# Attention scores by pairs of heads, in the two 64-row halves of the array

## The chip, the cores and the metric

The kernel runs on one core of a Trainium2 chip. The metric is the device time of one execution, in microseconds. Three runs of the kernel before gave 2763.35, 2765.78 and 2760.66 us, with a median of 2763.35 us. One more execution was recorded by the hardware profiler: 2758.38 us in all, of which the recorded span, from the first to the last instruction, is 2756.6 us. All durations below are from that one execution, so sums are made against it, and they are carried to the median by adding 5 us.

## The reference

The kernel computes one layer of an encoder: x is 2048 tokens by 1024 features in float32. A normalised x is multiplied by one large input matrix, which gives the operands of two token mixers (attention and an mLSTM) and two gates. Their outputs are projected, gated, multiplied by `w_out` and added to x; a feed-forward part of width 4096 and a last normalisation follow. The change is in the attention:

```python
# 8 heads of width 64; chunks of 64 tokens; own chunk and the 8 before it
scores = jnp.einsum('bclhd,bckhd->bchlk', qc, kband) * (1.0 / math.sqrt(d))
rel_idx = jnp.clip(rel, -MAX_REL_DIST, MAX_REL_DIST) + MAX_REL_DIST    # 256
scores = scores + rel_bias[:, rel_idx]
p = softmax(where(valid, scores, -1e30))
out = jnp.einsum('bchlk,bckhd->bclhd', p, vband)
```

Keys at a distance of 256 or more all get the same bias of their head, the last column of `rel_bias`.

## The kernel before

The tokens are four blocks of 512. Each matrix product is done with every float32 operand split in two parts, a high one (rounded to TensorE's float32r) and a low one (the remainder), and three products: high by high, high by low, low by high. The large products (`quad`, `product`, `token_tiles`, `down`) are matmuls of 128 rows by 128 columns on 512 moving columns. They use sums of blocks of weights and of activations, which ScalarE (ACT) and VectorE (DVE) form and split.

Every piece of work is a generator, and the class `Flow` runs them all in Python with a clock per engine. A `yield "pe", 500` gives that step's planned duration; the planner always issues the step that could start first by its clocks, and so writes out one fixed order of instructions for each engine. A step that waits for a buffer (`yield "get", pool, n`) or an event waits in this plan. On the chip the engines then run their orders with semaphores. The large products have priority 5 and the attention 1, so the parts of attention are placed between the large products. `mixers(0)` begins the attention of blocks 0 and 1, `mixers(2)` that of blocks 2 and 3.

Within a block, `attention` (L1072) fetches the values of a pair of heads, and then starts `head` for each of the 8 heads. A head's keys and queries come from DRAM by SP's DMA queue (`kfar`, `qfar`); 64 partitions hold the high part of the keys and the other 64 their low part, so that one matmul over 128 rows gives two of the products. The queries stand in both halves. `unit` takes two of the head's four tiles of 128 queries. `scores` (L1265) makes for each tile the products with up to 640 keys, in one or two matmul groups of up to 320 columns, one matmul for the high part of the queries and one for the low part:

```python
for x in range(halves):
    for y in range(2):
        nc.tensor.matmul(bks[x][:, :w], q[:, y, i * P:(i + 1) * P],
                         kf[:, f * P + x * w:f * P + x * w + w], start=y == 0, stop=y == 1)
```

DVE adds the bias and takes the maximum (L1283), ACT the exponential (L1289), and one of the two divides by the sum. `turn` (L1299) transposes the probabilities on TensorE in pieces of up to four 128-blocks (L1308) and splits them (L1311, L1313). `weigh` (L1186) multiplies them by the values (L1201): where a block of keys serves both query tiles, one matmul with 512 moving columns does both, else one with 256. ACT and DVE add the halves of the result (L1212 to L1219), which is then kept in DRAM or split in place.

The bias of a head is a table of 128 by 640 values, read by one DMA from a row of 768 numbers; GpSimd writes -1e30 into two corners (L1118, L1119).

In four places outside the attention `norm_mid` (L1988) adds the squares of a row block by two matmuls with ones, with a tile `part` of its own.

Of the kernel before, what the change touches and what calls it, by code (L numbers as in the profile page):

```python
# [28 lines left out]
P = 128  # L29
# [219 lines left out]
class Layer:  # L249
# [8 lines left out]
    def make_tiles(self, pool, psum):  # L258
# [6 lines left out]
        self.bias = Pool([f32(f"bias{i}", 640) for i in range(2)])  # L265
# [16 lines left out]
        self.part, self.onesr = f32r("part", T), f32r("onesr", 2)  # L282
# [33 lines left out]
    def setup_late(self):  # L316
# [13 lines left out]
        nc.vector.tensor_copy(self.onesr, self.ones)  # L330
        fl.put(self.temp, raw)
# [489 lines left out]
    def dense(self):  # L821
# [36 lines left out]
        for s in range(NS):  # L858
# [212 lines left out]
    def attention(self, b):  # L1071
# [6 lines left out]
        for j in range(4):  # L1078
            vs = yield "get", self.rpool, 1 if b == 0 else 2
# [8 lines left out]
            for i in range(2):  # L1088
                h = 2 * j + i
                k, q = yield "get", self.rpool, 2  # L1090
                fl.spawn(self.head(b, h, vs, k, q), 1)
            if j == 0:
                fl.set(B["begun"])
        fl.set(B["kq_all"])
        yield "wait", B["head_done"]
        fl.put(self.rpool, *pt)
    def head(self, b, h, vs, k, q):
        fl, nc, B = self.fl, self.nc, self.blk[b]
        j, rows = h // 2, slice(h % 2 * 64, h % 2 * 64 + 64)
        kf = k.bitcast(F32)  # L1100
        for n, x in ((0, b - 1), (1, b)):
            if x < 0:
                continue
            yield "wait", [self.k_ev[x, j]]
            yield "sp", 800, 2000
            for a in range(2):
                nc.sync.dma_start(kf[a * 64:a * 64 + 64, n], self.kfar[x].ap()[j, a, rows])
        yield "wait", [self.q_ev[b, j]]
        yield "sp", 800, 2000
        for a in range(2):  # L1110
            nc.sync.dma_start(q.bitcast(F32)[a * 64:a * 64 + 64],
                              self.qfar[b].ap()[j, :, rows].rearrange("a p c -> p a c"))
        (bias,) = yield "get", self.bias, 1
        yield "sp", 1500, 2000
        rb = self.io["rb"]
        nc.sync.dma_start(bias, bass.AP(rb.tensor, h * 768, [[1, P], [1, 640]]))
        yield "pool", 180
        nc.gpsimd.memset(bias[0:64, 0:64], NEG)  # L1118
        nc.gpsimd.memset(bias[64:128, 576:640], NEG)  # L1119
        done = [Event(), Event()]  # L1120
        for u in range(2):
            fl.spawn(self.unit(b, h, u, k, q, bias, done[u]), 1)
        yield "wait", done
        fl.put(self.bias, bias)
        fl.put(self.rpool, k, q)
        B["heads_left"][j] -= 1
        if B["heads_left"][j] == 0:
            fl.put(self.rpool, *vs)
        fl.set(B["head_done"][h])
# [20 lines left out]
    def unit(self, b, h, u, k, q, bias, done):  # L1150
# [3 lines left out]
        prob, evs = {}, []  # L1154
        for n in range(2):
            i = 2 * u + n
            evs.append(Event())
            prob[i] = sct[n]
            fl.spawn(self.scores(b, i, k, q, bias, sct[n], evs[n]), 1)
        first = {i: (4 if b == 0 else i) for i in prob}  # L1160
        i0 = 2 * u
        cols = []
        for kt in range(min(first.values()), i0 + 6):
            use = [i for i in prob if first[i] <= kt <= i + 4]
            cols.append((kt, use))
        cols.sort(key=lambda c: (-len(c[1]), c[0]))
        pieces, room = [], 0
        for c in cols:
            if room < len(c[1]):
                pieces.append([])  # L1170
                room = 4
            pieces[-1].append(c)
            room -= len(c[1])
# [3 lines left out]
        for n, pc in enumerate(pieces):  # L1177
            (slots[n],) = yield "get", B["pt"], 1
            fl.spawn(self.turn(pc, slots[n], prob, first, pev[n]), 1)
        fl.spawn(self.weigh(b, h, u, pieces, slots, pev, done), 1)  # L1180
# [3 lines left out]
    def weigh(self, b, h, u, pieces, slots, pev, done):  # L1184
        fl, nc, B = self.fl, self.nc, self.blk[b]
        i0 = 2 * u  # L1186
        yield "wait", [B["vp_ev"][h // 2]]
# [5 lines left out]
        for pc, sl, ev in zip(pieces, slots, pev):  # L1193
            yield "wait", [ev]
            yield "pe", sum((0, 116, 228)[len(use)] for _, use in pc)
            o = 0
            for kt, use in pc:
                st = self.v_part(b, h, kt)
                c0 = (use[0] - i0) * P
                w = len(use) * P  # L1200
                nc.tensor.matmul(bkv[:, :, c0:c0 + w], st, sl[:, :, o:o + w], start=n == 0,  # L1201
                                 stop=n == total - 1)
                n += 1
                o += w
# [3 lines left out]
        r0 = (h % 2) * 64  # L1208
        own, other = slice(r0, r0 + 64), slice(64 - r0, 128 - r0)
        (tmp,) = yield "get", self.temp, 1  # L1210
        yield "act", act_ns(512, True)
        nc.scalar.copy(tmp[own, :512], bk[other])  # L1212
        yield "dve", dve_ns(512)
        nc.vector.tensor_add(tmp[own, :512], bk[own], tmp[own, :512])  # L1214
        fl.put(self.banks, bk)
        cols = slice(u * 256, u * 256 + 256)
        direct = self.direct(b, h // 2)
        yield "dve", dve_ns(256)
        nc.vector.tensor_add(tmp[own, :256], tmp[own, :256], tmp[own, 256:512])  # L1219
        if direct:  # L1220
            yield "wait", [B["mix_got"]]
            r = B["mix"][h // 2]
            yield "act", act_ns(256)
            nc.scalar.copy(r[own, 0, cols], tmp[own, :256])  # L1224
            yield "dve", dve_ns(256)
            nc.vector.tensor_sub(r[own, 1, cols], tmp[own, :256], r[own, 0, cols].bitcast(F32))  # L1226
            fl.put(self.temp, tmp)
            self.mix_done(b, h // 2)
            fl.set(done)
            return  # L1230
        fl.spawn(self.keep_mix(b, h // 2, self.mixd.ap()[b, h // 2, own, cols], tmp[own, :256], self.temp, tmp), 1)
# [33 lines left out]
    def scores(self, b, i, k, q, bias, sct, ev):  # L1265
        fl, nc = self.fl, self.nc
        e, st = sct
        f = 4 if b == 0 else i
        n = (i + 5 - f) * P
        kf = k.rearrange("p a c -> p (a c)")  # L1270
        halves = 2 if n > 256 else 1
        w = n // halves
        bks = yield "get", self.banks, halves
        yield "pe", 500
        for x in range(halves):
            for y in range(2):
                nc.tensor.matmul(bks[x][:, :w], q[:, y, i * P:(i + 1) * P],  # L1277
                                 kf[:, f * P + x * w:f * P + x * w + w], start=y == 0, stop=y == 1)
        br = bias[:, ::-1]
        j0 = 640 - n  # L1280
        for x in range(halves):
            yield "dve", dve_ns(w)
            nc.vector.tensor_tensor_reduce(  # L1283
                out=e[:, x * w:x * w + w], in0=bks[x][:, :w], in1=br[:, j0 + x * w:j0 + x * w + w],
                op0=ALU.add, op1=ALU.min, scale=-1.0, scalar=st[:, 0:1] if x > 0 else 3e38, accum_out=st[:, x:x + 1])
            fl.put(self.banks, bks[x])
        mx = st[:, halves - 1:halves]
# [11 lines left out]
    def turn(self, piece, slot, prob, first, ev):  # L1299
        fl, nc = self.fl, self.nc  # L1300
        (bk,) = yield "get", self.banks, 1
        n = sum(len(use) for _, use in piece)
        yield "pe~", 108 * n
        o = 0
        for kt, use in piece:
            for i in use:
                c = (kt - first[i]) * P
                nc.tensor.transpose(bk[:, o:o + P], prob[i][0][:, c:c + P], self.ident)  # L1308
                o += P
        yield "act", act_ns(o, True)  # L1310
        nc.scalar.copy(slot[:, 0, :o], bk[:, :o])  # L1311
        yield "dve", dve_ns(o)
        nc.vector.tensor_sub(slot[:, 1, :o], bk[:, :o], slot[:, 0, :o].bitcast(F32))  # L1313
# [674 lines left out]
    def norm_mid(self, s, h):  # L1988
# [9 lines left out]
        yield "act", act_ns(512)  # L1998
        nc.scalar.copy(self.part, tot[:, :512])
        (bk,) = yield "get", self.banks, 1  # L2000
        for x in range(2):
            yield "pe", 227
            nc.tensor.matmul(bk, self.onesr[:, 0:1].to_broadcast([P, P]), self.part, start=x == 0, stop=x == 1,
                             skip_group_check=True)
            if x == 0:
                yield "dve", dve_ns(512)
                nc.vector.tensor_sub(self.part, tot[:, :512], self.part.bitcast(F32))
# [308 lines left out]
    def late(self):  # L2316
        yield from self.setup_late()
        self.fl.set(self.ev_late)

    def build(self):  # L2320
# [15 lines left out]
        self.gated, self.mtd = f32d("gatepart", 40, T), f32d("mrow", NB, MH, T)  # L2336
        self.fin_ev = [E(KT) for _ in range(2)]
# [129 lines left out]
```

## Time and profile before

| | |
|---|---|
| median of three runs | 2763.35 us |
| profiled execution, and its span | 2758.38 us, 2756.6 us |
| TensorE (PE) busy | 2725.7 us, 99% |
| weight loads (PEld) busy | 2265.7 us, 82% |
| VectorE (DVE) busy | 2098.2 us, 76% |
| ScalarE (ACT) busy | 1551.2 us, 56% |
| GpSimd (POOL) busy | 50.4 us, 2% |
| DMA queue of SP, share of 16 engines | 73.3% |
| scores, matmuls (L1277) | 480 |
| values, matmuls (L1201) | 336 |

A line such as "L1277 PE MATMUL bank<-r,r 128\*128 128x320 f32 x384" names the source line, the engine, the operation, what is written and read, the stationary tile (rows\*columns of the array), the moving tile (partitions x columns) and the count. In a group the mean duration of a matmul is from its issue to its end in PSUM; matmuls overlap in the pipeline, so what one costs the engine is the distance from its start to the next one's start, which the timeline gives. PEld is the loading of the stationary tile, which can go on while the matmul before still streams.

### The profile page before, as it was taken

How to read it: one execution, taken by the hardware profiler on the slowest of the kernel's cores; microseconds unless marked ns; L12 is line 12 of the kernel's file. 1: busy time of each engine (PE TensorE's matmuls, PEld its weight loads, DVE VectorE, ACT ScalarE, POOL GpSimd, SP SyncE). 2: the span in 40 equal slices, each digit the busy share in tenths (PEclk: the TensorE clock that was granted, in tenths of full speed). 3: DMA queues.
4: the chain of work that ended last, by engine and by line, in shares of the span. 5: the costliest groups of instructions: out<-in, count | busy, mean ns of one | idle time of the engine just before them, and what ended most of it. 6: DMA issues, size and time to landing. Idle time of an engine off the chain costs nothing.

```text
span 2756.6 us, 38227 instructions
## 1 busy us (share of the span) xinstructions
PE 2725.7 (99%) x12856; PEld 2265.7 (82%) x12856; DVE 2098.2 (76%) x3715; ACT 1551.2 (56%) x2665; POOL 50.4 (2%) x124
## 2 busy tenths in 40 slices
PE   9999999999999999999999999999999999999998
PEld 8878888788888888788888888888788888888887
DVE  7878766788886678897767898788888675667675
ACT  6555456757763435566556776576445565564443
POOL 0000000000000000000000000000000000000000
PEclk9999999999999999999999999999999999999999
DMA  8877678888978898757769876777665464578763
GB/s 296 287 265 258 237 258 279 254 267 275 293 257 272 305 317 305 256 204 262 261 236 295 253 255 213 245 225 259 219 230 178 153 217 154 187 259 276 283 228 129
DMA packets 331145, 682.46 MB, mean 248 GB/s; under 512 B 36708, under 2 KB 61924, under 8 KB 330948
## 3 DMA queue, kind: packets, MB, share of 16 engines
q1 hardware_dynamic: 330804, 680.01, 73.3%
q8 instruction: 101, 1.65, 0.2%
q14 instruction: 96, 0.79, 0.1%
q10 hardware_dynamic: 144, 0.01, 0.0%
HBM read 468.74 MB, written 211.14 MB: 247 GB/s over the span
## 4 chain that ended last, share of the span: by engine, by line
PE 88%; DVE 5%; issue 2%; ACT 2%; DMA 2%; POOL 0%; SPq 0%; POOLq 0%; ACTq 0%; DVEq 0%
PE bank L610 38%; PE bank L541 10%; PE bank L542 10%; PE bank L543 10%; PE bank L641 10%; PE bank L646 2%; PE bank L1201 2%; PE bank L1277 2%; PE bank L1308 2%; DVE wsp L482 1%; ACT wsp L480 1%; PE bank L1551 0%; ACT sc L1289 0%; DVE r L1065 0%; DMA r<-qfar 0%
## 5 line engine op out<-in xcount | busy, mean ns | idle before, releaser
L610 PE MATMUL bank<-r,wsp 128*128 128x512 f32 x4872 | 1113.2, 390 | 2.9 <-DVE ctx L1944 1.2
L610 PEld LDWEIGHTS bank<-r,wsp 128*128 128x128 f32 x4872 | 914.3, 188 | 195.4 <-DVE ctx L1944 1.6
L480 ACT CAST wsp<-wraw 128x1024 fp32r<-128x1024 f32 x453 | 475.8, 1051 | 479.8 <-PE bank L610 192.2
L482 DVE TENSOR_TENSOR wsp<-wraw,wsp 128x1024 fp32r<-128x1024 f32 x453 | 553.4, 1222 | 223.6 <-ACT wsp L480 215.4
L541 PE MATMUL bank<-r,wsp 128*128 128x512 f32 x1152 | 455.1, 395 | 0.4 <-ACT r L1224 0.4
L542 PE MATMUL bank<-r,wsp 128*128 128x512 f32 x1152 | 449.8, 390 | 0.0
L543 PE MATMUL bank<-r,wsp 128*128 128x512 f32 x1152 | 449.5, 390 | 0.0
L641 PE MATMUL bank<-r,wsp 128*128 128x512 f32 x1512 | 369.8, 394 | 1.2 <-DVE tmp L1214 1.2
L641 PEld LDWEIGHTS bank<-r,wsp 128*128 128x128 f32 x1512 | 278.6, 189 | 56.8 <-DVE tmp L1214 1.6
L543 PEld LDWEIGHTS bank<-r,wsp 128*128 128x128 f32 x1152 | 216.4, 188 | 46.1
L541 PEld LDWEIGHTS bank<-r,wsp 128*128 128x128 f32 x1152 | 216.7, 188 | 41.7 <-ACT r L1224 0.8
L542 PEld LDWEIGHTS bank<-r,wsp 128*128 128x128 f32 x1152 | 216.7, 188 | 40.6 <-DVE r L1226 0.2
L1065 DVE TENSOR_TENSOR r<-r 128x512 fp32r<-128x512 f32 x269 | 179.4, 686 | 67.8 <-ACT r L1060 66.6
L1060 ACT CAST r<-r 128x512 fp32r<-128x512 f32 x269 | 162.8, 620 | 110.7 <-DMA r<-u 88.6
L1737 DVE TENSOR_TENSOR ctx<-bank,ctx 128x512 f32<-128x512 f32 x150 | 102.8, 686 | 69.4 <-PE bank L610 69.1
L499 DVE TENSOR_TENSOR wraw<-wraw,wraw 128x1024 f32<-128x1024 f32 x112 | 136.1, 1218 | 1.8 <-DMA wsum<-wraw 0.6
L1289 ACT ACTIVATE sc<-sc,scs 128x640 f32<-128x640 f32 (+4 forms) x128 | 97.4, 761 | 62.6 <-DVE scs L1283 61.6
L1729 ACT COPY ctx<-bank 128x512 f32<-128x512 f32 x150 | 87.2, 582 | 53.6 <-PE bank L610 52.6
L2062 ACT ACTIVATE ctx<-ctx 128x512 f32<-128x512 f32 x96 | 60.5, 630 | 100.6 <-DVE ctx L1737 100.4
L1313 DVE TENSOR_TENSOR r<-bank,r 128x512 fp32r<-128x512 f32 (+1 forms) x168 | 96.5, 593 | 10.2 <-ACT r L1311 9.3
L1201 PE MATMUL bank<-r,r 128*128 128x512 f32 x336 | 97.5, 373 | 2.8 <-DVE r L1313 2.5
L1311 ACT CAST r<-bank 128x512 fp32r<-128x512 f32 (+1 forms) x168 | 80.9, 514 | 22.7 <-PE bank L1308 21.4
(243 smaller groups left out, 2994.5 us busy)
## 6 DMA issues: line engine op xcount, KB each, us to landing
wraw<-in_wf SPq DMA_DIRECT2D x202, 512.0 KB, 4.1
wraw<-wsum SPq DMA_DIRECT2D x120, 512.0 KB, 4.7
r<-u SPq DMA_DIRECT2D x224, 256.0 KB, 4.3
u<-ctx SPq DMA_DIRECT2D x128, 256.0 KB, 2.2
u<-tmp SPq DMA_DIRECT2D x96, 256.0 KB, 2.1
wraw<-in_w SPq DMA_DIRECT2D x47, 512.0 KB, 4.4
ctx<-in_wf SPq DMA_DIRECT2D x88, 256.0 KB, 4.6
wsum<-ctx SPq DMA_DIRECT2D x88, 256.0 KB, 4.0
```

The lines of the kernel that those rows point to most:

```text
L480: nc.scalar.copy(w[:, 0], raw)
L482: nc.vector.tensor_sub(w[:, 1], raw, w[:, 0].bitcast(F32))
L499: V.tensor_sub(dst, x, y)
L541: mm(ps, lh, rh, start=first, stop=False)
L542: mm(ps, lh, rl, start=False, stop=False)
L543: mm(ps, ll, rh, start=False, stop=last)
L610: mm(ps, wv[:, x, k, n], a[:, y], start=new and k == 0 and x == y == 0, stop=k == 3 and x == 1, skip_group_check=True)
L641: mm(ps, wv[:, x, k, n], a[:, y], start=start and x == y == 0, stop=stop and x == 1, skip_group_check=True)
L1060: self.nc.scalar.copy(dst[:, 0], src)
L1065: self.nc.vector.tensor_sub(dst[:, 1], src, dst[:, 0].bitcast(F32))
L1201: nc.tensor.matmul(bkv[:, :, c0:c0 + w], st, sl[:, :, o:o + w], start=n == 0, stop=n == total - 1)
L1737: nc.vector.tensor_add(t[:, o:o + 512], ps, t[:, o:o + 512])
```

## The change

One task now does a pair of heads. The keys' high parts of both heads are one tile (`kh`, head 0 in partitions 0 to 63, head 1 in 64 to 127), the low parts another (`kl`). The scores of a query tile are made for both heads at once: each product is a matmul over 64 rows, head 0 in rows 0 to 63 of the array and head 1 in rows 64 to 127, into two PSUM banks; three products per head. The keys are cut into the nearest 384 and what is left (up to 256), since only the nearest 384 have differing biases: the table loses the last column's value (softmax doesn't change by a constant), so the farther keys need only a mask. The table without that value is made at the start (`late`) and kept in DRAM. The values are weighed by one matmul of 256 moving columns per head and key block. Beside it, `norm_mid` takes a tile of the common pool for its split and has planner priority 0 in place of 3.

```diff
-        self.bias = Pool([f32(f"bias{i}", 640) for i in range(2)])
+        self.bias = Pool([f32(f"bias{i}", 768) for i in range(2)])
+        self.mask = f32("mask", 256)
...
-                        fl.spawn(self.norm_mid(s, h), 3)
+                        fl.spawn(self.norm_mid(s, h), 0)
...
+    def pair(self, b, j, vs, kh, kl, q):
...
+            for a, k in enumerate((kh, kl)):
+                yield "sp", 800, 2000
+                nc.sync.dma_start(k.bitcast(F32)[:, n], self.kfar[x].ap()[j, a])
...
+        nc.sync.dma_start(q.bitcast(F32), self.qfar[b].ap()[j].rearrange("a p c -> p a c"))
...
+        for x in range(2):
+            yield "sp", 1000, 2000
+            nc.sync.dma_start(bias[:, x], bass.AP(rb.tensor, (2 * j + x) * 512, [[1, P], [1, 384]]))
+            yield "pool", 120
+            nc.gpsimd.memset(bias[0:64, x, 0:64], NEG)
...
+        for i in range(NT):
+            fl.spawn(self.unit(b, j, i, kh, kl, q, bias, read[i], done[i]), 1)
...
-            yield "pe", sum((0, 116, 228)[len(use)] for _, use in pc)
...
-                nc.tensor.matmul(bkv[:, :, c0:c0 + w], st, sl[:, :, o:o + w], start=n == 0,
-                                 stop=n == total - 1)
+            yield "pe", 116 * len(pc)
+            for o, (kt, a) in enumerate(pc):
+                nc.tensor.matmul(bkv[:, :, a * P:a * P + P], self.v_part(b, 2 * j + a, kt), sl[:, :, o * P:o * P + P],
+                                 start=n == 0, stop=n == total - 1, skip_group_check=True)
...
-        halves = 2 if n > 256 else 1
...
-        yield "pe", 500
...
+        cuts = [(0, n)] if n <= 384 else [(0, n - 384), (n - 384, n)]
...
+        for x, (c0, c1) in enumerate(cuts):
+            w = c1 - c0
+            bks = yield "get", self.banks, 2
+            yield "pe", 3 * (0.42 * w + 13) + 130
+            for y, (u, v) in enumerate(((0, 0), (0, 1), (1, 0))):
+                for a in range(2):
+                    rows = slice(a * 64, a * 64 + 64)
+                    nc.tensor.matmul(bks[a][:, :w], q[rows, u, i * P:(i + 1) * P],
+                                     kf[v][rows, f * P + c0:f * P + c1], start=y == 0, stop=y == 2)
+            for a in range(2):
+                fl.spawn(self.row_max(n, x, c0, c1, bks[a], bias[:, a], sct[a], maxed[a], evs[a]), 1)
...
+    def late(self):
+        yield from self.setup_late()
+        (tab,) = yield "get", self.temp, 1
+        yield "sp", 60, 2000
+        self.nc.sync.dma_start(tab[:AH, :512], self.io["rb"])
+        yield "dve", dve_ns(512)
+        self.nc.vector.tensor_scalar(tab[:AH, :512], tab[:AH, :512], tab[:AH, 511:512], None, op0=ALU.subtract)
+        yield from self.store(self.rbd.ap(), tab[:AH, :512], Event(), self.temp, tab)
```

(In `late`, the call of `setup_late` is not new.)

More of the change, by code (lines that the diff above doesn't have):

```diff
@@ L1094, in attention @@
         fl.set(B["kq_all"])
-        yield "wait", B["head_done"]
+        yield "wait", B["pair_done"]
         fl.put(self.rpool, *pt)
-    def head(self, b, h, vs, k, q):
+    def pair(self, b, j, vs, kh, kl, q):
         fl, nc, B = self.fl, self.nc, self.blk[b]
-        j, rows = h // 2, slice(h % 2 * 64, h % 2 * 64 + 64)
-        kf = k.bitcast(F32)
         for n, x in ((0, b - 1), (1, b)):
@@ L1104, in head @@
             yield "wait", [self.k_ev[x, j]]
-            yield "sp", 800, 2000
-            for a in range(2):
-                nc.sync.dma_start(kf[a * 64:a * 64 + 64, n], self.kfar[x].ap()[j, a, rows])
+            for a, k in enumerate((kh, kl)):
+                yield "sp", 800, 2000
+                nc.sync.dma_start(k.bitcast(F32)[:, n], self.kfar[x].ap()[j, a])
         yield "wait", [self.q_ev[b, j]]
[L1109 to L1122, printed above, removed]
-        yield "wait", done
[L1124 to L1129, printed above, removed]
+        yield "sp", 1570, 2000
+        nc.sync.dma_start(q.bitcast(F32), self.qfar[b].ap()[j].rearrange("a p c -> p a c"))
+        (tile,) = yield "get", self.bias, 1
+        bias = tile.rearrange("p (a c) -> p a c", a=2)
+        rb = self.rbd.ap()
+        for x in range(2):
[3 more added lines that the diff above has]
+            nc.gpsimd.memset(bias[0:64, x, 0:64], NEG)
+        read, done = [Event() for _ in range(NT)], [Event() for _ in range(NT)]
+        for i in range(NT):
+            fl.spawn(self.unit(b, j, i, kh, kl, q, bias, read[i], done[i]), 1)
+        yield "wait", read
+        fl.put(self.bias, tile)
+        fl.put(self.rpool, kh, kl, q)
+        yield "wait", done
+        fl.put(self.rpool, *vs)
+        fl.set(B["pair_done"][j])
     def v_part(self, b, h, kt):
@@ L1149, in evac_v, with unit @@
         fl.put(self.banks, bk)
-    def unit(self, b, h, u, k, q, bias, done):
+    def unit(self, b, j, i, kh, kl, q, bias, read, done):
         fl, nc, B = self.fl, self.nc, self.blk[b]
         sct = yield "get", self.sc, 2
[L1154 to L1173, printed above, removed]
+        evs = [Event(), Event()]
+        yield from self.scores(b, i, (kh, kl), q, bias, sct, evs, read)
+        first = 4 if b == 0 else i
+        blocks = [(kt, a) for kt in range(first, i + 5) for a in range(2)]
+        pieces = [blocks[n:n + 4] for n in range(0, len(blocks), 4)]
         yield "wait", evs
@@ L1227, in weigh @@
             fl.put(self.temp, tmp)
-            self.mix_done(b, h // 2)
+            self.mix_done(b, j)
             fl.set(done)
             return
-        fl.spawn(self.keep_mix(b, h // 2, self.mixd.ap()[b, h // 2, own, cols], tmp[own, :256], self.temp, tmp), 1)
+        fl.spawn(self.keep_mix(b, j, self.mixd.ap()[b, j, :, cols], tmp[:, :P], self.temp, tmp), 1)
         fl.set(done)
@@ L1263, in take_mix, with scores @@
         self.fl.set(B["mix_got"])
-    def scores(self, b, i, k, q, bias, sct, ev):
+    def scores(self, b, i, k, q, bias, sct, evs, read):
+        fl, nc = self.fl, self.nc
+        f = 4 if b == 0 else i
+        n = (i + 5 - f) * P
+        cuts = [(0, n)] if n <= 384 else [(0, n - 384), (n - 384, n)]
+        kf = [x.rearrange("p a c -> p (a c)") for x in k]
+        maxed = [[Event() for _ in cuts] for _ in range(2)]
+        for x, (c0, c1) in enumerate(cuts):
[7 more added lines that the diff above has]
+                                     kf[v][rows, f * P + c0:f * P + c1], start=y == 0, stop=y == 2)
+            for a in range(2):
+                fl.spawn(self.row_max(n, x, c0, c1, bks[a], bias[:, a], sct[a], maxed[a], evs[a]), 1)
+        yield "wait", maxed[0] + maxed[1]
+        fl.set(read)
@@ L1266, in scores, with row_max @@
+    def row_max(self, n, x, c0, c1, bk, bias, sct, maxed, ev):
         fl, nc = self.fl, self.nc
         e, st = sct
-        f = 4 if b == 0 else i
-        n = (i + 5 - f) * P
-        kf = k.rearrange("p a c -> p (a c)")
-        halves = 2 if n > 256 else 1
-        w = n // halves
-        bks = yield "get", self.banks, halves
-        yield "pe", 500
[L1275 to L1287, printed above, removed]
+        if x > 0:
+            yield "wait", maxed[:1]
@@ L1288, in scores @@
+        w = c1 - c0
+        add = bias[:, ::-1][:, 384 - w:] if x == len(maxed) - 1 else self.mask[:, 256 - w:]
+        yield "dve", dve_ns(w)
+        nc.vector.tensor_tensor_reduce(
+            out=e[:, c0:c1], in0=bk[:, :w], in1=add,
+            op0=ALU.add, op1=ALU.min, scale=-1.0, scalar=st[:, 0:1] if x > 0 else 3e38, accum_out=st[:, x:x + 1])
+        fl.put(self.banks, bk)
+        fl.set(maxed[x])
+        if x < len(maxed) - 1:
+            return
+        mx = st[:, x:x + 1]
         yield "act", act_ns(n, ap=2)
@@ L1297, in scores, with turn @@
         fl.set(ev)
-    def turn(self, piece, slot, prob, first, ev):
+    def turn(self, piece, slot, sct, first, ev):
         fl, nc = self.fl, self.nc
         (bk,) = yield "get", self.banks, 1
[L1302 to L1313, printed above, removed]
+        n = len(piece) * P
+        yield "pe~", 108 * len(piece)
+        for o, (kt, a) in enumerate(piece):
+            nc.tensor.transpose(bk[:, o * P:o * P + P], sct[a][0][:, (kt - first) * P:(kt - first) * P + P], self.ident)
+        yield "act", act_ns(n, True)
+        nc.scalar.copy(slot[:, 0, :n], bk[:, :n])
+        yield "dve", dve_ns(n)
+        nc.vector.tensor_sub(slot[:, 1, :n], bk[:, :n], slot[:, 0, :n].bitcast(F32))
         fl.put(self.banks, bk)
@@ L1997, in norm_mid @@
         yield "wait", summed
-        yield "act", act_ns(512)
-        nc.scalar.copy(self.part, tot[:, :512])
+        (r,) = yield "get", self.rpool, 1
+        yield from self.split(tot[:, :512], r)
         (bk,) = yield "get", self.banks, 1
+        yield "pe", 454
         for x in range(2):
[L2002 to L2007, printed above, removed]
+            nc.tensor.matmul(bk, self.onesr[:, 0:1].to_broadcast([P, P]), r[:, x], start=x == 0, stop=x == 1)
+        fl.put(self.rpool, r)
         yield "dve", dve_ns(512)
```

66 lines of the change are left out of this document (31 added, 35 removed).

## The prediction

> **What bounds the kernel now.** I read the page's busy times first, then the windows of the two stretches in which the attention runs, then TensorE's timeline.
>
> ```profile
> PE 2725.7 (99%) x12856; PEld 2265.7 (82%) x12856; DVE 2098.2 (76%) x3715; ACT 1551.2 (56%) x2665; POOL 50.4 (2%) x124
> ```
> ```profile
> core 0: us, PE busy (x) PEld busy (x) DVE busy (x) ACT busy (x) POOL busy (x), PEclk, DMA share, GB/s
> 470.00:830.00 360.00, 351.37 (x1898) 295.80 (x1897) 297.87 (x791) 246.03 (x539) 18.70 (x48) 1.00 0.85 268
> 1500.00:1970.00 470.00, 464.11 (x2459) 394.31 (x2458) 403.07 (x973) 310.73 (x650) 19.44 (x51) 1.00 0.75 238
> sum 830.00, PE 815.49 PEld 690.11 DVE 700.93 ACT 556.76 POOL 38.14; mean PE 407.74 PEld 345.06 DVE 350.47 ACT 278.38 POOL 19.07
> ```
>
> TensorE is the bound over the span and in the attention's stretches, where it is busy 815.5 of 830 us at full clock. So a microsecond more or less on TensorE is nearly a microsecond of time, and at most 14.5 us of idle can be won back there. VectorE has 129 us to spare in these stretches, ScalarE 273 us.
>
> **What a matmul costs.** The chain of waits gives the widest sort, the timeline the others; I take the distance from one row's start to the next one's, divided by the count.
>
> ```profile
> 249.57 203.36 PE bank L610 x897
> ```
> ```profile
> 793.70 0.38 PE L1551 MATMUL bank<-ctx,ctx 128*128 128x129 f32 x2
> 793.91 0.39 PE L1553 MATMUL bank<-ctx,ctx 128*128 128x129 f32 x2
> ...
> 801.08 0.74 PE L1277 MATMUL bank<-r,r 128*128 128x320 f32 x4
> 801.66 2.91 PE L641 MATMUL bank<-r,wsp 128*128 128x512 f32 x12
> ...
> 813.53 0.40 PE L1201 MATMUL bank<-r,r 128*128 128x256 f32 x2
> 813.76 0.82 PE L1308 MATMUL bank<-const,sc 128*128 128x128 f32 x6
> ```
>
> 512 columns take 203.36 / 897 = 0.227 us, 320 take 0.58 / 4 = 0.145, 256 take 0.23 / 2 = 0.115, 129 take 0.21 / 2 = 0.105. From the first two, a column costs 0.43 ns; that gives 0.172 for 384 and 0.118 for 256. At 129 columns the streaming alone would be about 0.065; the rest I read as the weight load that each matmul brings, so about 0.107 us is the least for a matmul with its own weights (0.11 for 128 and 192 columns below).
>
> **The change, part by part.**
>
> *Scores before.*
>
> ```profile
> L1277 PE MATMUL bank<-r,r 128*128 128x320 f32 x384 | 73.2, 314 | 1.9 <-DVE scs L1283 1.8 <-DMA r<-qfar 0.2
> L1277 PE MATMUL bank<-r,r 128*128 128x256 f32 x48 | 9.1, 296 | 1.7 <-DVE scs L1283 1.2 <-DVE ctx L1592 0.5
> L1277 PE MATMUL bank<-r,r 128*128 128x192 f32 x32 | 4.9, 274 | 0.0
> L1277 PE MATMUL bank<-r,r 128*128 128x128 f32 x16 | 2.9, 264 | 0.0
> ```
>
> 384 x 0.145 + 48 x 0.118 + 48 x 0.11 = 55.7 + 5.7 + 5.3 = 66.7 us.
>
> *Scores after.* By the built order there are 336 matmuls of 384 columns, 312 of 256 and 48 of 128, all over 64 rows, alternating between the lower and the upper half. If the two of a pair run at once, a pair costs one matmul: 168 x 0.172 + 156 x 0.118 + 24 x 0.11 = 28.9 + 18.4 + 2.6 = 49.9 us. That is 16.8 us less. No row shows two halves at once, so the ends are 49.9 and, one after the other, 99.8. A middle case is that only the weight loads of the halves go in turn: 348 pairs x 2 x 0.107 = 74.5 us. I take 49.9: the timeline's loads already run beside the streaming of another matmul (the load of L1457 below starts 0.22 us before its matmul), and two halves share no cells.
>
> *Going to 64 rows and back.* This is what decides. In the built order the row-half matmuls stand in 114 separate groups (109 of six, three of twelve, one six in two parts), nearly all between full-array matmuls, so the array changes its form 228 times. The kernel before has small matmuls over 40 and 16 rows, and others over all rows with only 4 columns of weights:
>
> ```profile
> 145.36 1.52 PE L610 MATMUL bank<-r,wsp 128*128 128x512 f32 x6
> 146.81 0.44 PE L1337 MATMUL bank<-const,tmp 40*128 40x40 f32 x4
> 147.18 1.66 PE L610 MATMUL bank<-r,wsp 128*128 128x512 f32 x6
> ```
> ```profile
> 146.81 0.32 PEld L1337 LDWEIGHTS bank<-const,tmp 40*128 40x128 f32 x4 [0.35 <-issue]
> 147.18 1.46 PEld L610 LDWEIGHTS bank<-r,wsp 128*128 128x128 f32 x7
> ```
> ```profile
> 159.02 1.29 PE L610 MATMUL bank<-r,wsp 128*128 128x512 f32 x5
> 160.25 0.23 PE L1422 MATMUL bank<-const,cum 16*128 16x16 f32 x1
> 160.33 0.37 PE L1423 MATMUL bank<-const,cum 16*128 16x16 f32 x2
> 160.63 1.65 PE L610 MATMUL bank<-r,wsp 128*128 128x512 f32 x6
> ```
> ```profile
> 165.52 2.88 PE L610 MATMUL bank<-r,wsp 128*128 128x512 f32 x12
> 168.24 0.60 PE L1457 MATMUL bank<-const,g_mt 128*4 128x128 f32 x4
> 168.59 0.94 PE L610 MATMUL bank<-r,wsp 128*128 128x512 f32 x3
> ```
> ```profile
> 168.02 0.53 PEld L1457 LDWEIGHTS bank<-const,g_mt 128*4 128x4 f32 x4
> ```
>
> First place: six of 0.227 from 145.36 stream until 146.72. A lone one lasts 1.52 - 5 x 0.227 = 0.39 with its pipeline. The last of the six behind ends at 148.84, so it began at 148.45 and the first really at 147.32. Of the 0.60 between, the four small ones take 0.28 (their starts are (0.44 - 0.23) / 3 apart, with L1422's 0.23 as the length of a lone one): 0.32 us is lost. Second place, likewise: 160.15 to 160.76 is 0.61, less three of 0.107: 0.29 lost. At the third, over all rows, it is 168.24 to 168.69 for four of 0.107: 0.02 lost. The load rows say how: L1457's load starts 0.22 us ahead of its matmul, beside the streaming; L1337's load and the load of L610 behind it start with their matmul, so the engine first ran empty, and nothing covered the load. For a group of the change I take 0.35 us: the lower end is 0.29; the upper is 0.32 + 0.11 = 0.43, since the transposes' loads at L1337 are shorter than a 0.107 one. 114 x 0.35 = 39.9 us (33.1 to 49.0), all on the path, as TensorE itself waits.
>
> The Trainium skill (TensorEngine Tiling (Array Packing), Key Properties) says that a change of the tiling mode drains the engine, and that different tiles can load weights and multiply in parallel. For row tiles the trace agrees with the first (0.29 and 0.32 us); the narrow column tile lost 0.02 us, where the measurement decides. No run here shows the second; by it the forecast's 49.9 us of passes would stand, by loads in turn 74.5.
>
> *Values.*
>
> ```profile
> L1201 PE MATMUL bank<-r,r 128*128 128x512 f32 x224 | 75.1, 412 | 2.5 <-DVE r L1313 2.5
> L1201 PE MATMUL bank<-r,r 128*128 128x256 f32 x112 | 25.2, 295 | 0.2 <-ACT wsp L480 0.2
> ```
>
> Before 224 x 0.227 + 112 x 0.118 = 64.1; after 560 x 0.118 = 66.1: +2.0 us. The 560 transposes stay.
>
> *Other engines.*
>
> ```profile
> L1212 ACT COPY tmp<-bank 64x512 f32<-64x512 f32 x64 | 37.2, 582 | 24.0 <-PE bank L1201 22.6
> L1214 DVE TENSOR_TENSOR tmp<-bank,tmp 64x512 f32<-64x512 f32 x64 | 43.9, 686 | 8.1 <-ACT tmp L1212 7.0
> L1219 DVE TENSOR_TENSOR tmp<-tmp 64x256 f32<-64x256 f32 x64 | 26.7, 417 | 1.2
> L1224 ACT CAST r<-tmp 64x256 fp32r<-64x256 f32 x32 | 12.9, 403 | 20.9 <-DVE tmp L1219 20.3
> ```
>
> ACT: 64 copies become 128 of 256 columns, at most 128 x 0.403 = 51.6, so +14.4 at most. DVE: 128 x 0.417 + 64 of 128 columns (about 0.285) = 71.6 for 70.6. The maxima keep their columns (232 instructions for 240). All of this lies beside TensorE in the spare time above: 0; without that cover it would be up to 15 us.
>
> *Transfers.*
>
> ```profile
> r<-qfar SPq DMA_DIRECT2D x64, 256.0 KB, 5.4
> r<-kfar SPq DMA_DIRECT2D x112, 128.0 KB, 4.7
> bias<-in_rb SPq DMA_DIRECT2D x32, 320.0 KB, 5.1
> ```
>
> 208 issues on SP become 104 (56 for keys, 16 for queries, 32 for biases), with half the query bytes and 192 KB a bias; the results are kept in 36 issues for 32. GpSimd writes 32 corners for 64. A pair's first scores wait for seven transfers, as a head's did, and the second head for none. The attention waited for TensorE, not for these (0.2 us <-DMA r<-qfar above): 0. The setup's added load, subtraction and store come with the other constants, hundreds of microseconds before the attention's first stretch at 470 us: 0. `norm_mid` keeps its 8 matmuls: 0, in a stretch without attention; its place in the order may give or take the few us that its split lasts.
>
> *Idle.* A slower TensorE lets the others catch up; of the 14.5 us of idle I take 3 (0 to 8).
>
> Sum: -16.8 + 39.9 + 2.0 - 3 = +22.1 us. From the profiled 2758.4 that is 2780.5; the median of the runs stands 5 above the profiled one, so 2763.35 + 22.1 = 2785.5. The forecast's own ends are +10 and +34: 2773 to 2798.
>
> **Rivals.**
>
> *Loads in turn* (0.18): passes of 74.5, +24.6 on the sum: 2810. For it: within one form, loads never start less than 0.1 us apart. Against: no row has two different halves.
>
> *No overlap at all* (0.07): 99.8, +49.9: 2835.
>
> *Faster* (0.16): the loss at the small matmuls belongs to them (40 and 16 rows, four and three of them) and not to a change of form; groups of six long ones would not pay it. Then -16.8 + 2.0 - 3 = -17.8: 2745.5. Below 17.8 / 114 = 0.156 us a group, the change wins. Against: the loss is the same after 40 and 16 rows, and the third place, with equally small matmuls, has none.
>
> *No change* (0.09): a loss near 0.156 a group, as the diff's own plan has it (0.13): 2763.
>
> **How the numbers follow.** The forecast has 0.50. Slower is forecast, loads in turn and no overlap: 0.75; faster 0.16; within 0.2% (5.5 us, about what the measurement can tell) 0.09. The range 2745 to 2820 leaves out the last rival's 0.07 upward and half of the faster one downward.
>
> **What would show it.** In the changed profile a group of six should be followed and preceded by loads that start with their matmul; from the last start before to the first real start behind, a 384 group should take about 0.227 + 0.52 + 0.35. In a pair the two starts should lie almost together; if they lie 0.107 apart, loads go in turn; if 0.17 apart, there is no overlap. TensorE's busy time tells little, as its ends are modelled; starts decide. The forecast is wrong if groups lose under 0.2 us, or if TensorE's idle in the attention grows by tens of us.

## The result

The changed kernel took 2791.5 us (median of four runs, 2788.5 to 2797.5) against 2762.0 us for the kernel before: 29.5 us more, a ratio of 1.0113 with an interval of 1.0096 to 1.0129. The forecast was 2785.5 us, in a range of 2745 to 2820. The profiled execution took 2789.25 us, its span is 2787.5 us.

The first fence is from the page of the changed kernel, the second from its windows over the attention's two stretches (the columns are those of the same view before).

```profile
PE 2753.6 (99%) x13296; PEld 2258.1 (81%) x13296; DVE 2101.4 (75%) x3776; ACT 1549.6 (56%) x2713; POOL 44.2 (2%) x92
```
```profile
470.00:830.00 360.00, 353.02 (x2042) 285.59 (x2042) 288.62 (x799) 241.96 (x568) 14.11 (x32) 1.00 0.72 239
1500.00:1970.00 470.00, 461.39 (x2634) 373.27 (x2633) 390.10 (x990) 306.30 (x673) 16.90 (x39) 1.00 0.66 217
```

TensorE is still the bound and its idle in these windows is 15.6 us (14.5 before). VectorE and ScalarE have as much to do as before over the span (2101.4 for 2098.2 us, 1549.6 for 1551.2), and less in these windows. So the loss lies in what TensorE calls busy. The timeline shows one group of six half-array matmuls between full-array ones, the matmuls first and then the weight loads:

```profile
537.41 0.85 PE L644 MATMUL bank<-r,wsp 128*128 128x512 f32 x3
538.19 0.79 PE L1258 MATMUL bank<-r,r 64*128 64x384 f32 x6
538.91 1.66 PE L644 MATMUL bank<-r,wsp 128*128 128x512 f32 x6
```
```profile
537.30 0.54 PEld L644 LDWEIGHTS bank<-r,wsp 128*128 128x128 f32 x3
538.19 0.47 PEld L1258 LDWEIGHTS bank<-r,r 64*128 64x128 f32 x6 [0.35 <-DVE ctx L734]
538.91 1.45 PEld L644 LDWEIGHTS bank<-r,wsp 128*128 128x128 f32 x7 [0.25 <-issue]
```

Two narrower windows of the same views show the second full-array matmul behind the group, and the group's first two loads:

```profile
539.24 0.39 PE L644 MATMUL bank<-r,wsp 128*128 128x512 f32 x1
```
```profile
538.19 0.19 PEld L1258 LDWEIGHTS bank<-r,r 64*128 64x128 f32 x2 [0.35 <-DVE ctx L734]
```

Three things are to be seen. First, the group's first loads start with its first matmul (538.19), and so do those of the full-array matmuls behind it (538.91): nothing is loaded ahead across a change of form. Second, the three matmuls ahead stream until 537.41 + 3 x 0.227 = 538.09; the six behind end at 540.57, the last began 0.39 earlier and the first five steps of 0.227 before that, at 539.05. So the group holds TensorE for 0.96 us, of which three passes of 0.172 are 0.52: 0.44 us are lost by this reckoning. It rests on modelled ends; by starts alone the first full-array matmul really began 0.227 before the second, at 539.02, and 0.93 - 0.52 = 0.41 us are lost. These can be followed: 0.10 us from the end of the streaming to the first load (538.09 to 538.19), that load of 0.107, and the same two once more behind the last pass (from 538.30 three passes last until 538.81, the load starts at 538.91).

Third, the first two loads, of 0.18 us each, take 0.19 together, where in turn the second would start 0.107 later; all six take 0.47 us. The two halves load side by side.

### The profile page after: what moved, and what is told of

Same layout as the page of the kernel before. It is cut to its first block, busy times and chain, and to the rows that moved or that the text cites. A ratio compares the mean times of both kernels' runs of the same rounds, so it can differ in the third digit from the quotient of the medians.

```text
span 2787.5 us, 39049 instructions
## 1 busy us (share of the span) xinstructions
PE 2753.6 (99%) x13296; PEld 2258.1 (81%) x13296; DVE 2101.4 (75%) x3776; ACT 1549.6 (56%) x2713; POOL 44.2 (2%) x92
## 4 chain that ended last, share of the span: by engine, by line
PE 84%; DVE 6%; DMA 4%; issue 3%; ACT 2%; POOL 0%; SPq 0%; POOLq 0%; ACTq 0%; DVEq 0%
PE bank L613 37%; PE bank L644 10%; PE bank L544 9%; PE bank L545 9%; PE bank L546 9%; PE bank L1179 2%; PE bank L1258 2%; PE bank L649 2%; DMA r<-u 2%; PE bank L1298 1%; DVE wsp L485 1%; DVE r L1068 1%; DVE sc L1273 1%; ACT wsp L483 0%; PE bank L1525 0%
## 5 line engine op out<-in xcount | busy, mean ns | idle before, releaser
L544 PEld LDWEIGHTS bank<-r,wsp 128*128 128x128 f32 x1152 | 216.5, 188 | 45.6 <-issue 4.2
L1179 PE MATMUL bank<-r,r 128*128 128x256 f32 x560 | 102.1, 297 | 1.8 <-DVE r L1302 1.8
L1179 PEld LDWEIGHTS bank<-r,r 128*128 128x128 f32 x560 | 83.5, 190 | 19.2 <-issue 4.2
```

Source lines behind the costliest of these rows:

```text
L544: mm(ps, lh, rh, start=first, stop=False)
L1179: nc.tensor.matmul(bkv[:, :, a * P:a * P + P], self.v_part(b, 2 * j + a, kt), sl[:, :, o * P:o * P + P], start=n == 0, stop=n == total - 1 ...
```

## The experiments

Theory: two changes of form a group, at about 0.40 us together, are the loss, and the two halves do run at once. Rivals: the halves stream in turn; or the pairs, the cuts and the new order cost by themselves.

**Do the halves run at once?** Both heads on the lower half:

```diff
-                    rows = slice(a * 64, a * 64 + 64)
+                    rows = slice(0, 64)
```

> Both heads' score matmuls are put on rows 0 to 63 (head 1's scores are then those of head 0, so its part of the attention is left out); counts, shapes and order stay. If the two halves run at once, as their starts 3 to 4 ns apart say, this doubles the passes: 49.9 us more than the changed kernel's 2791.5, about 2841 us, and the starts of a pair lie 0.17 us apart for 384 columns. If the starts are only recorded together and the halves stream in turn anyway, the time stays at 2791.

It took 2824.9 us, 33.4 more than the changed kernel. The same group in its timeline:

```profile
540.40 0.86 PE L644 MATMUL bank<-r,wsp 128*128 128x512 f32 x3
541.19 1.31 PE L1258 MATMUL bank<-r,r 64*128 64x384 f32 x6
542.43 1.89 PE L644 MATMUL bank<-r,wsp 128*128 128x512 f32 x7
```

Six matmuls last 1.31 us here and 0.79 in two halves: 0.52 more, which is three passes of 0.172. So two halves do stream at once, at the price of one. Over all groups that is 49.9 us of TensorE, but the time rose by only 33.4; the expected 2841 was too high. The two profiled executions show part of the reason: TensorE is busy for 47.4 us more (2801.0 for 2753.6), and its idle falls from 33.9 to 23.3 us, as the busier engine waits less for the others.

**Full rows in the pairs.** The operands of each head stacked as before the change, in the changed kernel's pairs, cuts and order:

```diff
-            kq = yield "get", self.rpool, 3
+            kq = yield "get", self.rpool, 4
...
-            yield "pe", 3 * (0.42 * w + 13) + 130
-            for y, (u, v) in enumerate(((0, 0), (0, 1), (1, 0))):
-                for a in range(2):
-                    rows = slice(a * 64, a * 64 + 64)
-                    nc.tensor.matmul(bks[a][:, :w], q[rows, u, i * P:(i + 1) * P],
-                                     kf[v][rows, f * P + c0:f * P + c1], start=y == 0, stop=y == 2)
+            yield "pe", 4 * (0.42 * w + 13)
+            for a in range(2):
+                for y in range(2):
+                    nc.tensor.matmul(bks[a][:, :w], q[a][:, y, i * P:(i + 1) * P],
+                                     kf[a][:, f * P + c0:f * P + c1], start=y == 0, stop=y == 1)
```

> The changed kernel with its pairs, cuts, biases and order, but with the scores over all 128 rows (high and low part of a head's keys stacked, two matmuls of full rows per head and cut, as before). If the changes of form are the whole loss: no such change is left, scores 66.7 us and values 66.1, so 2762 + 2 = 2764 us, with the idle at most 2769. If the pairs, the cuts or the new order cost by themselves, it stays above 2780.

It took 2788.9 us: no change of form is left, and almost nothing was won. By this run alone the theory would have fallen. But the kernel differs in more than the form: the queries of each head stand twice, so a pair holds four operand tiles in place of three, with more transfers, and the plan's price of a group is another, so the order differs too. What the profile shows is idle and a lower clock; the windows of its span's late part, and two matmuls in it:

```profile
core 0: us, PE busy (x) PEld busy (x) DVE busy (x) ACT busy (x) POOL busy (x), PEclk, DMA share, GB/s
1900.00:2000.00 100.00, 88.62 (x451) 75.16 (x451) 86.77 (x207) 59.91 (x117) 0.29 (x2) 0.91 0.60 192
1966.80:1977.00 10.20, 6.50 (x27) 6.17 (x28) 8.31 (x32) 7.11 (x15) 0.00 (x0) 0.50 0.55 185
```
```profile
1987.14 0.63 PE L544 MATMUL bank<-r,wsp 128*128 128x512 f32 x1
1987.57 0.63 PE L545 MATMUL bank<-r,wsp 128*128 128x512 f32 x1
```

TensorE stands idle for 11 of 100 us, and its granted clock is 0.91 on average there: 0.50 for 10.2 us, and again from 1983.9 for 6.8 us, where two matmuls of 512 columns start 0.43 us apart for the 0.227 elsewhere.

**Taking the changes of form away, and nothing else.** The changed kernel's tiles, transfers, plan and order, with three full-row matmuls in place of six halves:

```diff
-            for y, (u, v) in enumerate(((0, 0), (0, 1), (1, 0))):
-                for a in range(2):
-                    rows = slice(a * 64, a * 64 + 64)
-                    nc.tensor.matmul(bks[a][:, :w], q[rows, u, i * P:(i + 1) * P],
-                                     kf[v][rows, f * P + c0:f * P + c1], start=y == 0, stop=y == 2)
+            for a, u, v in ((0, 0, 0), (0, 0, 1), (1, 1, 0)):
+                nc.tensor.matmul(bks[a][:, :w], q[:, u, i * P:(i + 1) * P],
+                                 kf[v][:, f * P + c0:f * P + c1], start=a == 1 or v == 0, stop=a == 1 or v == 1,
+                                 skip_group_check=True)
```

> The changed kernel in its own order, with its tiles, transfers and plan, but each group of six half-array matmuls is three over all 128 rows (two into one head's bank, one into the other's; so the scores are not those of the reference). The streaming is the same 49.9 us, and the 228 changes of form are gone. If these cost 0.40 us a group, 114 x 0.40 = 45.6 us fall away: 2791.5 - 45.6 = 2746 us, and up to 2758 where idle elsewhere takes some back. If the pairs and their order are what costs, as the 2788.9 us with full rows may say, it stays above 2775.

It took 2743.2 us, 48.3 less than the changed kernel; 48.3 / 114 = 0.42 us a group. The same group, and its loads:

```profile
532.26 0.85 PE L644 MATMUL bank<-r,wsp 128*128 128x512 f32 x3
532.95 0.69 PE L1256 MATMUL bank<-r,r 128*128 128x384 f32 x3
533.47 1.78 PE L644 MATMUL bank<-r,wsp 128*128 128x512 f32 x7
```
```profile
532.72 0.59 PEld L1256 LDWEIGHTS bank<-r,r 128*128 128x128 f32 x3
533.29 1.76 PEld L644 LDWEIGHTS bank<-r,wsp 128*128 128x128 f32 x8
```

Now the loads come 0.23 and 0.18 us ahead of the matmuls (532.72 for 532.95, 533.29 for 533.47). By the first reckoning above the group holds TensorE from 532.94 to 533.50, 0.56 us, against 0.96: 0.40 us less. The other groups between 512-column matmuls agree: by the starts of single matmuls in the two traces, a group of 384 columns holds 0.92 us in the changed kernel and 0.54 here (medians of 19 and 17), one of 256 columns 0.76 and 0.37 (9 and 10).

**Four passes in the same tiles.** As the last one, with two full-row matmuls per head (the lines taken out are those above):

```diff
+            for a in range(2):
+                for v in range(2):
+                    nc.tensor.matmul(bks[a][:, :w], q[:, a, i * P:(i + 1) * P],
+                                     kf[v][:, f * P + c0:f * P + c1], start=v == 0, stop=v == 1)
```

> The changed kernel with its three operand tiles, transfers and plan, and four matmuls over all rows per group, as many passes as before the change (the scores mix the two heads). From three full-row passes (2743.2 us) one pass of four more is 16.8 us: 2760 us, that is the kernel before. Then pairs, cuts and values cost nothing together, and the 2788.9 us with full rows came from that kernel's fourth operand tile and its transfers. If the pairs with four passes cost by themselves, 2775 to 2790.

It took 2756.3 us, a ratio of 0.9981 to the kernel before (0.9972 to 0.9991). So with the kernel before's number of passes, all the rest of the change costs nothing and wins some 6 us. The full-row kernel's 2788.9 is not the price of pairs, cuts or values: it comes from what sets these two kernels apart (in the profiles, 45.1 us of idle there and 27.2 here). Their last score matmuls start at the end of the range that each line gives, first the four-tile kernel:

```profile
L1262 PE MATMUL bank<-r,r x464: 220/333/688, 480.6 to 1980.6; 128*128 128x384 f32 x77, 128*128 128x256 f32 x66, 128*128 128x128 f32 x12
```
```profile
L1257 PE MATMUL bank<-r,r x464: 218/333/441, 476.4 to 1907.1; 128*128 128x384 f32 x74, 128*128 128x256 f32 x69, 128*128 128x128 f32 x12
```

With four tiles the attention's last scores come 73 us later. Whether the scarce tiles, the added transfers or the other price in the plan delay them was not tried apart.

**Adding changes of form.** One more small matmul ahead of the third product of each group, into unused columns of a bank, once over all rows (shown) and once over rows 0 to 63. The kernel makes 116 groups, of which a few stand side by side; hence 114 separate ones above:

```diff
+                if y == 2:
+                    nc.tensor.matmul(bks[0][:, 384:512], q[:, 0, i * P:(i + 1) * P], kf[0][:, f * P + c0:f * P + c0 + P],
+                                     start=True, stop=True, skip_group_check=True)
...
```

> The changed kernel with one more matmul in each of the 116 groups, 128 columns over all rows, put ahead of the third product into unused columns of the bank: each group then has two changes of form more. If a pair of changes costs 0.40 us, with about 0.05 us of streaming beside it: 116 x 0.45 = +52 us, 2825 to 2845 us (some may be taken up by idle). If a change of form costs nothing, at most what the next kernel shows.

> The same added matmul at the same place, but over rows 0 to 63, so that no change of form is added: by its streaming and load 0.05 to 0.11 us each, +6 to +13 us: 2797 to 2805 us by either theory.

They took 2828.2 and 2805.3 us: 36.7 and 13.8 more than the changed kernel. The first lies in the expected range; the second is at its upper edge. In its timeline (the first fence; the second is over all rows) the third product lasts 0.44 us: its two halves, of 0.33 and 0.39 us, start 0.05 apart in the trace and no longer together.

```profile
539.37 0.61 PE L1261 MATMUL bank<-r,r 64*128 64x384 f32 x4
539.82 0.22 PE L1257 MATMUL bank<-r,r 64*128 64x128 f32 x1
539.83 0.44 PE L1261 MATMUL bank<-r,r 64*128 64x384 f32 x2
```
```profile
539.65 0.61 PE L1261 MATMUL bank<-r,r 64*128 64x384 f32 x4
540.19 0.33 PE L1257 MATMUL bank<-r,r 128*128 128x128 f32 x1
540.45 0.44 PE L1261 MATMUL bank<-r,r 64*128 64x384 f32 x2
```

Over all rows the added matmul starts 0.54 us after the start of its group (540.19 from 539.65), over 64 rows 0.45; the third product follows it by 0.26 us in place of 0.01. That is 0.34 us for two changes of form, 39 us over 116 groups. The times of the two kernels lie only 22.9 us apart; here too, not all of TensorE's loss reached the time, and TensorE's idle is 27.4 us with the added changes and 35.4 without.

**One part alone, in the kernel before.** A small matmul ahead of each of its 128 score groups, over 64 rows and over 128:

```diff
+        nc.tensor.matmul(bks[0][:, :P], q[0:64, 0, i * P:(i + 1) * P], kf[0:64, f * P:f * P + P], start=True, stop=True,
+                         skip_group_check=True)
         for x in range(halves):
```

> The kernel before with one added matmul of 128 columns over 64 rows ahead of each of its 128 score groups, overwritten by the group's first matmul: two changes of form each. At about 0.42 us a pair of changes and 0.05 of streaming: 128 x 0.47 = 60 us on TensorE, of which idle takes up to 17: 2805 to 2822 us. If the small matmul is the cost and not the form, as with the next kernel.

> The same added matmul over all 128 rows: no change of form. 128 x 0.107 = 13.7 us on TensorE at most: 2766 to 2776 us by either theory.

They took 2801.0 and 2782.6 us, 39 and 20.6 more than the kernel before: the first less than expected, the second more. Their timelines, 64 rows first:

```profile
629.83 1.07 PE L641 MATMUL bank<-r,wsp 128*128 128x512 f32 x4
630.83 0.32 PE L1275 MATMUL bank<-r,r 64*128 64x128 f32 x1
631.08 0.85 PE L1279 MATMUL bank<-r,r 128*128 128x320 f32 x4
631.77 1.53 PE L641 MATMUL bank<-r,wsp 128*128 128x512 f32 x6
```
```profile
624.69 1.30 PE L641 MATMUL bank<-r,wsp 128*128 128x512 f32 x5
625.84 0.22 PE L1275 MATMUL bank<-r,r 128*128 128x128 f32 x1
625.89 0.80 PE L1279 MATMUL bank<-r,r 128*128 128x320 f32 x4
626.53 1.78 PE L641 MATMUL bank<-r,wsp 128*128 128x512 f32 x7
```

From the end of the streaming ahead (630.74 and 625.83) to the next full matmul are 1.03 and 0.70 us; less four score matmuls of 0.145, the small one costs 0.45 us over 64 rows and 0.12 over 128. So the cost lies in the form and not in the size of the matmul: 0.33 us of difference at one size. Times 128, the small matmuls take 58 and 15 us of TensorE; the times moved by 39 and 20.6. On TensorE the theory holds here too, but the time doesn't follow TensorE one to one: 18.4 us of time lie between the two kernels for 42 of TensorE. In the profiles the idle is 23.7 us with 64 rows and 37.8 with 128, against 30.9 in the kernel before, so idle takes up a part of it.

**Fewer groups.** Both cuts of a query tile issued together, with four banks taken at once (78 groups for 114):

```diff
+        got = yield "get", self.banks, 2 * len(cuts)
+        yield "pe", 3 * (0.42 * n + 13 * len(cuts)) + 130
...
-            bks = yield "get", self.banks, 2
-            yield "pe", 3 * (0.42 * w + 13) + 130
+            bks = got[2 * x:2 * x + 2]
...
```

> The changed kernel with the two cuts of a query tile issued together, with four banks taken at once: 78 groups of row-half matmuls in place of 114, with the same matmuls. If each group pays 0.40 us, 36 fewer give -14 us: 2777 us (2774 to 2783, as waiting for four banks may take some back). If the loss is not paid by the group, 2791.

It took 2829.6 us: worse by 38, where 14 less were expected. Fewer changes of form were paid for with waiting. Its windows for 1600 to 1800 us, and one group of twelve (256 columns, then 384) in its timeline:

```profile
1600.00:1800.00 200.00, 182.23 (x977) 148.59 (x976) 151.92 (x412) 113.73 (x271) 10.23 (x20) 0.91 0.57 191
```
```profile
704.03 1.29 PE L644 MATMUL bank<-r,wsp 128*128 128x512 f32 x5
705.25 1.15 PE L1259 MATMUL bank<-r,r 64*128 64x256 f32 x12
706.33 1.87 PE L644 MATMUL bank<-r,wsp 128*128 128x512 f32 x7
```

TensorE is idle for 18 of 200 us at a mean clock of 0.91. Over the span it is idle for 58.1 us (33.9 in the changed kernel); its longest waits are those of value products for split probabilities (9.6 us) and of transposes for the division (9.6 and 6.2 us). That the banks, of which a tile's scores hold four at once here, cause them is likely, not shown. So the time of this run says nothing on the price of a group, but its timeline does: the group holds TensorE from 705.17 to 706.45, 1.28 us, of which six passes are 3 x (0.118 + 0.172) = 0.87. The rest, 0.41 us, is the price of one trip for both cuts; apart, in the changed kernel, they hold 0.76 + 0.92 = 1.68 us. The loss is paid by the trip, as the theory has it, and not by the matmul or the pass.

**The planner's priority** of `norm_mid`:

```diff
-                        fl.spawn(self.norm_mid(s, h), 0)
+                        fl.spawn(self.norm_mid(s, h), 3)
```

> The changed kernel with the planner's priority 3 for the added-up squares, as before. It stands outside the attention and TensorE shows no idle there: within 3 us of 2791. If the priority costs by moving the order, 2785 or less.

It took 2792.2 us (2788.8 to 2797.7), within 1 us of the changed kernel: this part does nothing to the time that could be told from the scatter.

**A version that beats both.** Since four passes in pairs won some 6 us, the early return of buffers was tried alone in the kernel before; the second kernel has besides it a planned price nearer to the trace:

```diff
-        yield "wait", done
+        yield "wait", read
         fl.put(self.bias, bias)
         fl.put(self.rpool, k, q)
+        yield "wait", done
...
             fl.put(self.banks, bks[x])
+        fl.set(read)
```
```diff
-        yield "pe", 500
+        yield "pe", 2 * (0.42 * n + 13 * halves) + 15
```

> The kernel before with one thing of the change alone: a head gives its key, query and bias buffers back when its scores are out of the banks, and not when its values are weighed; full rows as before. Four passes with the pairs' early release took 2756.3 us for 2762.0. If the early release is what makes the rest of the change a little faster, 2750 to 2758 us here, faster than both kernels. If it is the pairs or their transfers, 2762.

> The same, with the plan's price of a tile's scores set to the 0.58 us that the trace shows (0.50 before). Within 4 us of the kernel without it, if the plan's price matters little; the four-pass kernel in pairs gives no sign of more.

They took 2755.0 us (ratio to the kernel before 0.9969, 0.9956 to 0.9981) and 2758.1 us (0.9981, 0.9972 to 0.9990). The first is faster than both kernels of the case, by 0.3% against the one before; the second is within the expected 4 us of it. So the small gain that the rest of the change brings can be had by the early release alone, without pairs. That it is the same gain is not shown, nor where it arises: the profiled execution of the first took 2758.07 us, the slowest of its five, and its idle is 32.3 us for 30.9 before.

## Why the prediction was right

*Direction and size.* Slower was forecast with 0.75, by 22.1 us; it was 29.5.

*TensorE as the bound* was right for the sign. That a microsecond on TensorE is nearly one of time was too simple: 49.9 us of added streaming cost 33.4, and 58 us of small matmuls with their changes 39, while the 45.6 us (114 x 0.40) of the change itself came back in full (48.3) when they were taken away. In the profiles the first two have 10.6 and 7.2 us less idle than the kernels they were made from, and the third 1.9 less. Which waits shrink, and why they didn't grow again in the third, is open.

*Passes.* That the halves run at once was an assumption without a row; it was right (0.79 against 1.31 us for six), and their loads do so too (two in 0.19 us, six in 0.47). Both rivals of these, loads in turn and no overlap, are out. One reading given for loads in turn was wrong from the start: at L1337, in the row that the prediction shows, four loads of 0.14 us each take 0.32 together, so they start 0.06 us apart and not at least 0.1.

*The price of a group* is the step that was mis-sized: 0.35 us was taken, 0.42 was measured by the time (48.3 / 114) and about 0.39 by the starts, near the upper end of 0.43. In the first place of the kernel before, the loads into the small group start 0.06 us apart and are the shorter ones; with float32r weights of 128 columns a load of 0.107 stands open both into the group and out of it. In us: 39.9 forecast, 48.3 measured, 8.4 too few. This is more than the 7.4 by which the sum missed. The sign that was named, about 1.10 us from the last start before a 384 group to the first real start behind, came out at 1.15 (537.86 to 539.02).

*The rest* of the sum, passes, values and idle, was -16.8 + 2.0 - 3 = -17.8 us; the kernel with three passes and no change of form is 18.5 us under the kernel before (2743.2 to 2761.7). That this fits so closely is in part luck. One pass of four was worth 13.1 us of time (2756.3 less 2743.2) and not 16.8; and with four passes, where values and idle should have given 2.0 - 3 = -1 us, the kernel is 5.7 us under the one before. The 3 us of idle were not won either (15.6 for 14.5 us in the windows). The early return of the buffers, which alone was worth 8.6 us in the kernel before (2755.0 for 2763.6), has no term in the sum. The transfers, the setup and `norm_mid` at nothing were right (2792.2 with the old priority).

*The faster rival* is what the change would have been without the change of form: forecast at 2745.5, seen at 2743.2 with three full-row passes in place of the halves. The point from which it decides, 0.156 us a group, was passed by more than twice.

## What to carry to other kernels

Half-array matmuls do share the array for the price of one, but a trip from full rows to half rows and back costs about 0.4 us. Three passes in place of four save 0.12 to 0.17 us a group. By these numbers the halves would pay only if some three or four such groups stand in a row, or if the work around them has the same form; this is an estimate, and no run here has such a row. Putting two groups together did save a trip, but the waiting that came with it cost more. Before such a change, look for any small matmul of fewer rows in the profile: the place where its weight load starts together with its matmul gives a first idea of the price (0.29 and 0.32 us here, for 0.39 to 0.42 in the change).

When a part is undone to find its price, keep tiles, transfers, plan and order: the undo that added one buffer per pair, its transfers and another price in the plan hid 33 us of gain (2788.9 in place of 2756.3) behind idle and a lower clock of its own.

## What the runs showed of the hardware that was not expected

Weight loads into the two row halves run side by side: two of 128 columns in 0.19 us, and the six of a group in 0.47. A change between full rows and 64 rows stops the loading ahead in both directions (0.23 and 0.18 us ahead without it, 0 with it) and costs 0.33 us even for a matmul of equal size, while a change to four columns over all rows cost 0.02. The price is that of the trip: two groups put together paid 0.41 us once. And idle of a tenth in a stretch of 100 to 200 us came with a mean granted clock of 0.91 there: in one such stretch the clock was 0.50 for 10.2 us and again for 6.8, and two matmuls of 512 columns then started 0.43 us apart in place of 0.227.
